# Sample keys loaded by pairs of sequences in 1 KB pieces, scored in one run, with early loads tied to the gate

## The chip, the cores and the metric

The kernel runs on one core of a Trainium2 chip. The core has a matmul engine (TensorE, PE in the profile, with its weight loads listed apart as PEld), a vector engine (VectorE, DVE), an engine for activations and copies (ScalarE, ACT), a general engine (GpSimd, POOL) and an engine that here only issues DMAs (SyncE, SP). Each engine runs its own instructions strictly in order and waits on semaphores for the others. DMAs are issued from the queues of SP (the weights) and of POOL (nearly all the rest) and share 16 DMA engines. The metric is the device time of one execution in microseconds.

## The reference

One inference step of a decoder layer for a prompt (1 sequence of 256 tokens) and a sample group (8 sequences of 4 tokens), with model width 2048, all in float32. The parts, in order: a projection to the inputs of two branches, a Mamba-2 (SSD) branch and a gated linear attention (GLA) branch, sigmoid gates that merge the two, cross-attention into 256 memory tokens, and a causal ConvFFN of width 5632. The change concerns the cross-attention of the sample group and what is loaded for it during the gate. That part of the reference is

```python
def _cross_attend(hn, mem_k, mem_v, w_cq, w_co):
    q = (hn @ w_cq).reshape(Bsz, L, CROSS_HEADS, CROSS_HEAD_DIM)
    s = jnp.einsum('blhd,bmhd->bhlm', q, mem_k) * (CROSS_HEAD_DIM ** -0.5)
    pr = jax.nn.softmax(s, axis=-1)
    o = jnp.einsum('bhlm,bmhd->blhd', pr, mem_v)
    return o.reshape(Bsz, L, D_MODEL) @ w_co
```

There are 4 heads of width 512. The prompt's memory keys and values are computed in the same step; those of the eight sample sequences are inputs (`cache_mem_k`, `cache_mem_v`, each 8 x 256 x 4 x 512), 4 MB of keys and 4 MB of values per head.

## The kernel before, in words

**Layout.** Activations lie with channels on the 128 partitions and the 288 tokens (256 of the prompt, then 32 of the sample group) along the free axis. Every large product is done in three passes: the weights and the activations are split into a rounded high part and a remainder, and high x high, high x low and low x high are summed. ScalarE writes the high part of a weight tile (`whi`, line 107), VectorE the remainder (`wlo`, line 109); both come in rings of five tiles. Raw weights (`raw`) come from SP's queue in 512 KB tiles, in a ring of three. One such tile of a projection of 256 columns serves 24 matmuls of 288 columns.

**Stages.** Memory keys and values of the prompt; input projection with the SSD and GLA scans woven in; output projections of the branches into `mb`; the gate stage (`gate_b`, which merges the branches, two channel tiles for each projection); the mix projection (`w_mix_out`), which adds the residual and writes `h_d`; the cross-attention; the output projection `w_co`; the ConvFFN.

**Order.** A planner puts the instructions of each engine in an order of its own, by a simulated time; within that, the code hands it the work woven together: `weave(main, bg, n_main, n_bg)` advances the background generator in proportion to the main one. In the cross-attention the main generator of head `hd` is the query projection of head `hd + 1` (16 steps of 12 matmuls), for the last head the first twelve steps of `w_co` (144 matmuls); the background generator is `attend(hd)`, with 20 steps. The DMAs that POOL issues for the attention are kept in program order.

**Loads of the attention.** `mem_load` takes a tile of 128 x 1024 floats from a ring of ten (`k4`, 40 KB a partition in all). A tile of sample keys holds one sequence: four DMAs of 128 KB put the four quarters of the head's 512 channels on four groups of 32 partitions, 128 channels (512 bytes) to a piece. A key tile is then turned by blocks of 32 x 32 on VectorE (`turn_keys`, two instructions of 512 columns), so that a partition holds a channel. Prompt keys (`kp`) and prompt values (`vp`) have tiles of their own; values of sequences 4 to 7 (`vc`) take tiles of the ring, those of sequences 0 to 3 (`vq`) a large buffer shared with other stages. Keys of head 0 are asked for in the gate stage, one sequence for every two gate tiles, `kp`, `vp` and `vq` in the mix stage. Nothing there but the ring ties a load to a time.

**Scores of the sample group.** A query tile of the projection is 128 channels x 32 rows. `diag` copies it into the block-diagonal tile `xqm` (one block of 32 columns per sequence, zero outside the sequence's own four). For each sequence and each of the four channel quarters a matmul with 32 stationary columns adds 256 scores; four sequences lie side by side on TensorE's columns. This is done in two halves: sequences 0 to 3, after which the values of 4 to 7 are loaded into their tiles, and sequences 4 to 7, after which keys 0 to 4 of the next head are. Key 5 follows the split of the prompt values, keys 6 and 7, `kp`, `vp` and `vq` follow the value products (line 1505).

The functions that the change touches are below.

Of the kernel before, what the change touches and what calls it, by code (L numbers as in the profile page):

```python
# [8 lines left out]
F32 = mybir.dt.float32  # L9
# [7 lines left out]
P = 128  # L17
# [25 lines left out]
def hybrid_step(ctx: ExitStack, tc: tile.TileContext, I: dict, O: list):  # L43
# [1218 lines left out]
    def mem_load(hd, kind, b=0):  # L1262

        t = pk.tile([P, 1024], F32, tag="k4", bufs=10, name={"k": "kc", "kp": "kp", "vp": "vp", "v": "vc"}[kind])
        if kind in ("k", "kp"):
            src = I["cache_mem_k"][b, :, hd, :] if kind == "k" else o_pmk[0, :, hd, :]
            for i in range(4):
                tc.keep_in_program_order(G.dma_start(
                    out=t[32 * i:32 * i + 32].rearrange("p (t x) -> p t x", x=P),
                    in_=src[:, i * P:(i + 1) * P].rearrange("(t m) x -> m t x", m=32)))  # L1270
        else:
            src = I["cache_mem_v"][b, :, hd, :] if kind == "v" else o_pmv[0, :, hd, :]
            tc.keep_in_program_order(G.dma_start(out=t.rearrange("p (m d) -> p m d", m=2),
                                                 in_=src.rearrange("(m p) d -> p m d", p=P)))
        ktiles[hd, kind, b] = t

    turned = set()

    def turn_keys(hd, kind, b=0):

        if (hd, kind, b) not in turned:
            turned.add((hd, kind, b))
            t = ktiles[hd, kind, b]
            for c in range(2):
                V.transpose(t[:, 512 * c:512 * c + 512], t[:, 512 * c:512 * c + 512])
# [17 lines left out]
    def gate_b(t, a):  # L1303
# [5 lines left out]
        if t % 2:  # L1309
            mem_load(0, "k", t // 2)  # L1310
# [35 lines left out]
    for j2 in range(KT // 2):  # L1346
# [6 lines left out]
        if j2 < 2:  # L1353
            mem_load(0, ("kp", "vp")[j2])
        elif j2 < 6:
            vq_load(0, j2 - 2)
# [17 lines left out]
    xqm = [px.tile([P, 4, NB, NS], F32, name=f"xqm{i}") for i in range(2)]  # L1374
# [16 lines left out]
    def q_proj(hd):  # L1391
# [5 lines left out]
        def evac(j):  # L1397
            if j % 2 == 0:
                qp.append((q2("qh"), q2("ql")))
            qs = px.tile([P, T], F32, tag="qs", bufs=1, name="qs")  # L1400
            V.tensor_tensor(qs, accs[j][:, 0:T], rc[0], ALU.mult)
            split(qp[j // 2][0][:, j % 2, :], qp[j // 2][1][:, j % 2, :], qs[:, 0:SEQ])
            diag(xqm[hd % 2][:, j], qs[:, SEQ:T])
# [20 lines left out]
    def keys(t):  # L1424
        return t.rearrange("p (t j m) -> p j t m", t=8, j=4)

    def attend(hd):

        xq = xqm[hd % 2]
        more = hd < 3  # L1430
        ssc = la_tile()

        def scores(q):
            for d in range(4):
                for j in (3, 2, 1, 0):
                    b = 4 * q + j
                    MM(ssc[NS * j:NS * j + NS, 0:256], xq[:, d, b, :], keys(ktiles[hd, "k", b])[:, d], start=(q == 0 and d == 0),
                       stop=(q == 1 and d == 3))

        for b in (4, 5):  # L1440
            turn_keys(hd, "k", b)
            yield
        scores(0)
        for b in range(4, NB):
            mem_load(hd, "v", b)
        yield
        for b in (6, 7):
            turn_keys(hd, "k", b)
            yield
        turn_keys(hd, "kp")  # L1450
        kh, kl = r4("kTh"), r4("kTl")
        kv = keys(ktiles[hd, "kp", 0])
# [25 lines left out]
        vp = ktiles[hd, "vp", 0].rearrange("p (m d) -> p m d", m=2)  # L1478
        vh, vl = v2("vph"), v2("vpl")
        split(vh, vl, vp)  # L1480
        if more:
            mem_load(hd + 1, "k", 5)
# [26 lines left out]
        if more:  # L1509
            for b in (6, 7):  # L1510
                mem_load(hd + 1, "k", b)
# [283 lines left out]
```

## Time and profile before

| | us |
|---|---|
| median of three runs | 2558.97 (2555.58 to 2562.18) |
| the profiled execution | 2558.26 |
| its span, first to last instruction | 2556.5 |
| TensorE busy | 2514.2 |
| VectorE busy | 1749.1 |
| ScalarE busy | 1332.6 |
| POOL busy | 459.4 |
| last GLA output projection and start of the gate | about 1195 to 1240 |
| gate, mix | up to about 1425 |
| cross-attention, first query matmul to last fold | 1424.8 to 1631.3 |

The profile is of one execution. Its views are a page, groups of instructions by line, waits, the DMA queues (q0 is POOL's, q1 SP's: packets, MB, share of the 16 engines), instructions in order of time, and busy time by stretches. In a row of the order of time stand the start and the length in us, the engine, the line, the operation, the tile written and the tiles read, the count, and in brackets the idle time before it with what ended it. In a row of groups stand count, busy us, mean ns, and idle time before. Matmuls overlap, so a length of 0.29 us does not mean that a matmul costs as much.

### The profile page before, as it was taken

How to read it: one execution, taken by the hardware profiler on the slowest of the kernel's cores; microseconds unless marked ns; L12 is line 12 of the kernel's file. 1: busy time of each engine (PE TensorE's matmuls, PEld its weight loads, DVE VectorE, ACT ScalarE, POOL GpSimd, SP SyncE). 2: the span in 40 equal slices, each digit the busy share in tenths (PEclk: the TensorE clock that was granted, in tenths of full speed). 3: DMA queues.
4: the chain of work that ended last, by engine and by line, in shares of the span. 5: the costliest groups of instructions: out<-in, count | busy, mean ns of one | idle time of the engine just before them, and what ended most of it. 6: DMA issues, size and time to landing. Idle time of an engine off the chain costs nothing.

```text
span 2556.5 us, 50096 instructions
## 1 busy us (share of the span) xinstructions
PE 2514.2 (98%) x18678; PEld 2412.1 (94%) x18678; DVE 1749.1 (68%) x3712; ACT 1332.6 (52%) x2680; POOL 459.4 (18%) x849
## 2 busy tenths in 40 slices
PE   9999999999999999999999999899999999999998
PEld 8889999989999999998999988799999999999998
DVE  6656777787767666765765567567777677675765
ACT  7656547645364555544454543356545455454545
POOL 3002234241200000012101155412010101020010
PEclk9999999999999999999999999999999999999999
DMA  8776587776868585778757699655555555555553
GB/s 265 218 223 200 170 243 212 226 209 191 233 195 286 175 255 165 245 235 245 213 180 250 199 288 284 216 170 173 167 173 168 173 167 174 168 170 171 169 172 128
DMA packets 435812, 521.93 MB, mean 204 GB/s; under 512 B 28860, under 2 KB 375836, under 8 KB 435504
## 3 DMA queue, kind: packets, MB, share of 16 engines
q1 hardware_dynamic: 399536, 422.34, 54.6%
q0 software_dynamic: 36000, 96.38, 12.8%
q8 instruction: 146, 2.39, 0.4%
q14 instruction: 98, 0.80, 0.1%
q10 hardware_dynamic: 32, 0.01, 0.0%
HBM read 473.13 MB, written 45.48 MB: 203 GB/s over the span
## 4 chain that ended last, share of the span: by engine, by line
PE 92%; DMA 4%; DVE 1%; POOL 1%; ACT 1%; issue 0%; SPq 0%; DVEq 0%; ACTq 0%; POOLq 0%
PE acc L152 25%; PE acc L151 25%; PE acc L155 25%; PE acc L319 2%; PE acc L320 2%; PE acc L323 2%; DMA raw<-in_w_in_dram 1%; PE acc L1417 1%; PE acc L1418 1%; PE acc L1419 1%; DMA kc<-in_cache_mem_k_dram 1%; PE mm L1151 1%; PE la L1142 1%; DMA raw<-in_w_cq_dram 1%; DMA raw<-in_w_gla_out_dram 1%; PE mm L1115 1%
## 5 line engine op out<-in xcount | busy, mean ns | idle before, releaser
L109 DVE TENSOR_TENSOR wlo<-raw,whi 128x512 fp32r<-128x512 f32 x1464 | 994.8, 687 | 656.0 <-ACT whi L107 645.4
L107 ACT CAST whi<-raw 128x512 fp32r<-128x512 f32 x1464 | 894.0, 618 | 1048.3 <-PE acc L152 741.2
L151 PE MATMUL acc<-xn,whi 128*128 128x288 f32 (+1 forms) x1936 | 550.3, 299 | 1.1 <-ACT whi L107 1.1
L152 PE MATMUL acc<-xn,whi 128*128 128x288 f32 (+1 forms) x1936 | 541.8, 295 | 0.0
L155 PE MATMUL acc<-xn,wlo 128*128 128x288 f32 (+1 forms) x1936 | 414.2, 295 | 0.0
L152 PE MATMUL acc<-hf,whi 128*128 128x288 f32 x1408 | 393.2, 295 | 0.0
L151 PE MATMUL acc<-hf,whi 128*128 128x288 f32 x1408 | 389.0, 292 | 0.0
L151 PEld LDWEIGHTS acc<-xn,whi 128*128 128x128 f32 (+1 forms) x1936 | 364.1, 188 | 11.7 <-issue 8.3
L152 PEld LDWEIGHTS acc<-xn,whi 128*128 128x128 f32 (+1 forms) x1936 | 364.4, 188 | 6.8 <-issue 4.8
L155 PEld LDWEIGHTS acc<-xn,wlo 128*128 128x128 f32 (+1 forms) x1936 | 310.3, 188 | 1.8 <-issue 1.1
L155 PE MATMUL acc<-hf,wlo 128*128 128x288 f32 x1408 | 294.5, 290 | 0.0
L152 PEld LDWEIGHTS acc<-hf,whi 128*128 128x128 f32 x1408 | 264.5, 188 | 0.1
L151 PEld LDWEIGHTS acc<-hf,whi 128*128 128x128 f32 x1408 | 264.0, 188 | 0.1
L155 PEld LDWEIGHTS acc<-hf,wlo 128*128 128x128 f32 x1408 | 226.2, 188 | 0.0
L152 PE MATMUL acc<-pr,whi 128*128 128x288 f32 x704 | 196.6, 295 | 0.0
L151 PE MATMUL acc<-pr,whi 128*128 128x288 f32 x704 | 195.0, 293 | 0.0
L1619 POOL COPY fsp<-fst 128x16 f32<-128x16 f32 x88 | 36.5, 416 | 650.4 <-DVE av L1631 426.8
L151 PE MATMUL acc<-un,whi 128*128 128x288 f32 x512 | 146.1, 301 | 7.2 <-DVE mb L959 5.7
L155 PE MATMUL acc<-pr,wlo 128*128 128x288 f32 x704 | 147.4, 290 | 0.0
L152 PE MATMUL acc<-un,whi 128*128 128x288 f32 x512 | 143.0, 295 | 0.0
L152 PEld LDWEIGHTS acc<-pr,whi 128*128 128x128 f32 x704 | 132.3, 188 | 0.0
L151 PEld LDWEIGHTS acc<-pr,whi 128*128 128x128 f32 x704 | 132.0, 188 | 0.0
(504 smaller groups left out, 4369.5 us busy)
## 6 DMA issues: line engine op xcount, KB each, us to landing
raw<-in_w_in_dram SPq DMA_DIRECT2D x240, 512.0 KB
raw<-in_w_up_dram SPq DMA_DIRECT2D x176, 512.0 KB
raw<-in_w_down_dram SPq DMA_DIRECT2D x88, 512.0 KB
raw<-in_w_cv_dram SPq DMA_DIRECT2D x32, 512.0 KB
raw<-in_w_ssd_out_dram SPq DMA_DIRECT2D x32, 512.0 KB
sin<-in_state_gla_dram POOLq DMA_DIRECT2D x32, 512.0 KB, 6.0
out_dram<-sin SPq DMA_DIRECT2D x32, 512.0 KB
raw<-in_w_gla_out_dram SPq DMA_DIRECT2D x32, 512.0 KB
```

The costliest lines, as they stand in the source:

```text
L107: S.copy(view(hi), raw)
L109: V.tensor_tensor(view(lo), raw, view(hi), ALU.subtract)
L151: MM(a, hi[:, k, cs], xh, start=(k0 + s0 + k == 0), stop=False)
L152: MM(a, hi[:, k, cs], xl, start=False, stop=False)
L155: MM(a, lo[:, k, cs], xh, start=False, stop=(k0 + s0 + k == nk - 1))
L319: MM(accs[m], mn_hi[:, kk, ms_], hi[:, 0, :], start=(kk == 0), stop=False)
L320: MM(accs[m], mn_lo[:, kk, ms_], hi[:, 0, :], start=False, stop=False)
L323: MM(accs[m], mn_hi[:, kk, ms_], lo[:, 0, :], start=False, stop=(kk == KT - 1))
L1115: MM(a, kt[:, i, k * P:(k + 1) * P], vt[i], start=True, stop=True)
L1142: MM(osa[NS * j:NS * j + NS, :], qdm[:, k, b, :], sins[b][:, k, :], start=False, stop=(q == 1 and k == 0))
L1151: MM(a, kb[:, k * P:(k + 1) * P], vst, start=True, stop=True)
L1619: G.tensor_copy(sp[:, :, 0:2], st.rearrange("p (b k) -> p b k", k=2))
```

## The change

- **Ring.** Ten tiles of 1024 columns become five of 2048 (`k8`). A key tile holds a pair of sequences, the prompt keys and prompt values of a head share one tile (`kvp`), and two sequences' values share one.
- **Pieces.** A key tile is filled by four DMAs of 256 KB: two sequences by two channel halves, each on 32 partitions, 256 channels (1 KB) to a piece. A partition group thus belongs to one sequence and one half of the channels. The turn is the same, in instructions of 1024 columns.
- **Scores.** A matmul covers a pair of sequences and 64 channels, eight steps for the 512 channels, four pairs side by side. All pairs are done in one run, and after it the values of sequences 4 to 7 and the first two key pairs of the next head are asked for. The third pair follows the split of the prompt values, the fourth and the prompt's rows follow the value products. The last two key pairs are turned at the start of the head that uses them, the first two in the head before.
- **Queries.** The layout needs query channels on other partitions than the projection leaves them. `evac` writes the 32 sample columns of each query tile to `qsm`; `spread` multiplies them by two 0/1 tiles `perm` (two products per head) and two copies put the result into `xqm`. The copies by `diag` go.
- **Early loads.** The four key pairs of head 0 are asked for after gate tiles 3, 7, 11 and 15, and before each a one-column copy on POOL from that gate tile into the key tile makes the load wait for it. Prompt rows and `vq` are asked for in the mix stage, as before, `vq` one step earlier.
- **Steps.** `attend` has 18 steps in head 0 and 22 in the others.

```diff
+    def ring(name):
+        return pk.tile([P, 2048], F32, tag="k8", bufs=5, name=name)
+    def key_load(hd, c, after=None):
+        t = ktiles[hd, "k", c] = ring("kc")
+        if after is not None:
+            G.tensor_copy(t[:, 0:1], after)
+        for s_ in range(2):
+            for dh in range(2):
+                r = 64 * s_ + 32 * dh
+                tc.keep_in_program_order(G.dma_start(
+                    out=t[r:r + 32].rearrange("p (t x) -> p t x", x=256),
+                    in_=I["cache_mem_k"][2 * c + s_, :, hd, 256 * dh:256 * dh + 256].rearrange("(t m) x -> m t x", m=32)))
+    def rows_load(hd):
+        t = ktiles[hd, "p"] = ring("kvp")
...
+    def turn32(t, c):
+        V.transpose(t[:, 1024 * c:1024 * c + 1024], t[:, 1024 * c:1024 * c + 1024])
...
-        if t % 2:
-            mem_load(0, "k", t // 2)
+        if t % 4 == 3:
+            key_load(0, t // 4, th[:, 0:1])
...
-            V.tensor_tensor(qs, accs[j][:, 0:T], rc[0], ALU.mult)
-            split(qp[j // 2][0][:, j % 2, :], qp[j // 2][1][:, j % 2, :], qs[:, 0:SEQ])
-            diag(xqm[hd % 2][:, j], qs[:, SEQ:T])
+            V.tensor_tensor(qsm[:, j], accs[j][:, SEQ:T], rc[0][:, SEQ:T], ALU.mult)
+            V.tensor_tensor(qs, accs[j][:, 0:SEQ], rc[0][:, 0:SEQ], ALU.mult)
+            split(qp[j // 2][0][:, j % 2, :], qp[j // 2][1][:, j % 2, :], qs)
...
+    def spread(xq):
+        a = mm_tile()
+        for jh in range(2):
+            MM(a[:, jh * P:(jh + 1) * P], perm[jh].rearrange("p s d x -> p (s d x)"), qsm.rearrange("p j t -> p (j t)"),
+               start=True, stop=True)
+        for s_ in range(2):
+            rows = slice(64 * s_, 64 * s_ + 64)
+            f, g = xq[rows].rearrange("p j c t -> p (j c t)"), a[rows, 0:256]
...
     def attend(hd):
+        spread(xq)
+        yield
+        if hd:
+            for c in (2, 3):
+                for h_ in range(2):
+                    turn32(ktiles[hd, "k", c], h_)
+                    yield
         ssc = la_tile()
...
-        scores(0)
-        for b in range(4, NB):
-            mem_load(hd, "v", b)
...
-        scores(1)
-        if more:
-            for b in range(5):
-                mem_load(hd + 1, "k", b)
+        for j in range(8):
+            for c in (3, 2, 1, 0):
+                kt = ktiles[hd, "k", c].rearrange("p (t j m) -> p j t m", t=8, j=8)
+                MM(ssc[NS * c:NS * c + NS, 0:256], xq[:, j, c, :], kt[:, j], start=(j == 0), stop=(j == 7))
+        for c in (2, 3):
+            val_load(hd, c)
+        if more:
+            for c in (0, 1):
+                key_load(hd + 1, c)
...
-        weave(main, attend(hd), 16 if hd < 3 else 12, 20)
+        weave(main, attend(hd), 16 if hd < 3 else 12, 22 if hd else 18)
```

More of the change, by code (lines that the diff above doesn't have):

```diff
@@ L1430, in attend @@
         more = hd < 3
-        ssc = la_tile()
[L1433 to L1442, printed above, removed]
-        scores(0)
-        for b in range(4, NB):
-            mem_load(hd, "v", b)
+        spread(xq)
[5 more added lines that the diff above has]
+                    yield
+        ssc = la_tile()
+        for j in range(8):
[7 more added lines that the diff above has]
+                key_load(hd + 1, c)
         yield
[L1447 to L1450, printed above, removed]
+        yield
+        kp = ktiles[hd, "p"]
+        turn32(kp, 0)
         kh, kl = r4("kTh"), r4("kTl")
-        kv = keys(ktiles[hd, "kp", 0])
+        kv = kp[:, 0:1024].rearrange("p (t j m) -> p j t m", t=8, j=4)
         for d2 in range(2):
```

73 lines of the change are left out of this document (35 added, 38 removed).

## The prediction

> **What bounds the kernel now.** I read the page first, then the busy time by stretches, then the waits, the DMA queues and the order of time inside the two stretches that the change touches.
>
> ```profile
> span 2556.5 us, 50096 instructions
> PE 2514.2 (98%) x18678; PEld 2412.1 (94%) x18678; DVE 1749.1 (68%) x3712; ACT 1332.6 (52%) x2680; POOL 459.4 (18%) x849
> PE 92%; DMA 4%; DVE 1%; POOL 1%; ACT 1%; issue 0%; SPq 0%; DVEq 0%; ACTq 0%; POOLq 0%
> ```
>
> TensorE is the bound: 98% busy, 92% of the chain that ended last. A change that leaves its arithmetic alone can only win back time in which TensorE stands still or runs at a lower clock, so the question is where it does so. By stretches (length, then busy us and instruction count of PE, PEld, DVE, ACT, POOL; the granted clock; the DMA share; GB/s):
>
> ```profile
> 1195.00:1200.00 5.00, 5.00 (x40) 5.00 (x40) 2.62 (x6) 1.13 (x2) 2.36 (x4) 1.00 1.01 372
> 1200.00:1205.00 5.00, 4.60 (x35) 4.36 (x34) 0.00 (x0) 0.00 (x0) 1.75 (x3) 1.00 1.06 270
> 1205.00:1210.00 5.00, 2.01 (x15) 2.04 (x16) 2.03 (x4) 1.14 (x2) 3.64 (x7) 1.00 1.08 260
> 1200.00:1220.00 20.00, 14.31 (x104) 13.69 (x104) 7.25 (x14) 4.56 (x8) 11.52 (x20) 1.00 1.07 268
> 1220.00:1240.00 20.00, 18.86 (x134) 17.58 (x133) 10.73 (x22) 7.94 (x16) 4.81 (x9) 1.00 0.94 238
> 1240.00:1260.00 20.00, 20.00 (x154) 20.00 (x154) 18.08 (x33) 10.21 (x19) 0.57 (x1) 1.00 0.74 215
> 1424.80:1631.30 206.50, 191.43 (x1549) 166.25 (x1547) 128.98 (x276) 82.61 (x164) 89.33 (x146) 0.98 0.85 249
> 1520.00:1540.00 20.00, 18.05 (x144) 15.03 (x143) 15.39 (x39) 10.01 (x22) 12.12 (x21) 1.00 1.02 260
> 1600.00:1620.00 20.00, 11.83 (x112) 9.46 (x110) 13.11 (x30) 5.27 (x12) 5.18 (x8) 0.91 0.81 298
> 1605.00:1631.30 26.30, 17.18 (x126) 12.38 (x126) 13.25 (x31) 6.69 (x16) 3.01 (x6) 0.87 0.45 175
> ```
>
> A stretch with nothing in the way holds 154 matmuls in 20 us, 0.130 us each (1240 to 1260). The two rows ahead of it, where the last GLA output projection goes over into the gate stage, hold 104 and 134: 70 short, 70 x 0.130 = 9.1 us lost. The cross-attention (1424.8 to 1631.3) loses 206.5 - 191.4 = 15.1 us idle, and a mean clock of 0.98 is another 4 us: about 19 us. Of that the end of the last head (last row) has 9.1 us idle and 26.3 x 0.13 = 3.4 us by the clock, 12.5 together; 1600 to 1620, with 11.8 us busy of 20, is the worst of it. So 28 us at most are to be had.
>
> What ends the wait at the gate: ScalarE, which splits the weights, waits for raw weight tiles (us in total, times, longest), while the queue of POOL moves 32 key tiles:
>
> ```profile
> ACT whi L107 <- DMA raw<-in_w_in_dram: 12.3, 4, 4.2
> ACT whi L107 <- DMA raw<-in_w_gla_out_dram: 12.1, 2, 8.4
> q0 software_dynamic: 1854, 5.59, 60.8%
> q1 hardware_dynamic: 3677, 3.65, 44.6%
> kc<-in_cache_mem_k_dram POOLq DMA_DIRECT2D x32, 128.0 KB, 7.1
> ...
> mar<-mg_d POOLq DMA_DIRECT2D x1, 576.0 KB, 8.6
> ```
>
> The middle three rows are the DMA view of 1195 to 1228, the last is that of 1192 to 1200: POOL's queue (q0) takes 60.8% of the engines, the weights (q1) get 3.65 MB in 33 us, 111 GB/s. TensorE eats one 512 KB tile in 24 matmuls, 24 x 0.130 = 3.1 us, 168 GB/s. That is the loss.
>
> In the cross-attention the key loads again hold the queue. DMA view of 1474 to 1502 (all 4.2 MB of one head's keys), then of 1502 to 1521 (prompt rows and values, 2 KB pieces), then the value issues of the first head (KB, us to landing):
>
> ```profile
> q0 software_dynamic: 1527, 4.20, 60.6%
> q1 hardware_dynamic: 1366, 2.63, 36.1%
> ...
> q0 software_dynamic: 1472, 5.15, 75.0%
> q1 hardware_dynamic: 936, 1.82, 27.5%
> ...
> vc<-in_cache_mem_v_dram POOLq DMA_DIRECT2D x3, 512.0 KB, 9.5
> ```
>
> Keys in 512-byte pieces: 4.20 MB / 28 us = 150 GB/s at a 0.606 share, 247 GB/s if they had all engines. Pieces of 2 KB: 5.15 / 19 = 271 GB/s at 0.75, 361 GB/s. So the piece length has a price of its own. In the last head this arrives too late:
>
> ```profile
> 1460.76 1.43 POOL L1273 DMA_DIRECT2D vc<-in_cache_mem_v_dram  x2 [29.14 <-PE la L1437]
> 1493.03 1.16 POOL L1268 DMA_DIRECT2D kc<-in_cache_mem_k_dram  x2 [0.45 <-DMA kc<-in_cache_mem_k_dram]
> 1601.48 1.93 PE L1437 MATMUL la<-kc,xqm 128*32 128x256 f32 x32
> 1609.72 3.37 PE L1437 MATMUL la<-kc,xqm 128*32 128x256 f32 x32 [4.80 <-DVE kc L1285]
> 1620.12 0.72 PE L1494 MATMUL mm<-ident,prp 128*128 128x128 f32 x4 [2.61 <-DVE prp L1386]
> 1624.17 0.41 PE L1522 MATMUL mm<-pTh,vph 128*128 128x256 f32 x1
> ```
>
> At 1609.7 TensorE waits 4.8 us for the last keys; by then the output projection that was to run beside the head has been used up, so softmax, transposes and values follow one another bare, and the matmuls go at the lower clock (0.41 us where L1522 has 0.28 elsewhere).
>
> **The change, part by part.** *Gate.* The 32 key DMAs of head 0 become 16 of 256 KB, and each group of four waits behind a one-column POOL copy of a gate tile (t = 3, 7, 11, 15). In the order of instructions of the changed kernel the copies stand on POOL between the loads of the staged merge tiles, and the first h_d store comes after all of them. Gate tiles are two projections apart, 16 x 12 matmuls x 0.130 = 25 us, so 1 MB comes every 25 us instead of 4 MB at once. What stays at the old place are the staged loads mar and hx, 2 x 576 and 3 x 288 KB, 2.0 MB. Bounds of the gain: 9.1 us if they cause none of the loss, 0 if they cause all. TensorE was full up to 1200 (40 matmuls in 5 us), with these loads under way since 1192, and short from 1205, when only keys were left (15); I take 8, near the upper end. Four bursts of 1 MB beside 168 GB/s of weights: at a 0.6 share each starves the weights by some 60 GB/s for 5.5 us, 2 us of weights, which the ring of three tiles (9.4 us) covers; without that cover it is at most 4 x 2 us. VectorE's turns of those keys stand seven weight splits behind the gate tile, about 11 us; copy, issue and landing take some 9 (four issues of 0.58 and the 7.1 above). Nothing, but close.
>
> *Pieces of 1 KB.* Between 247 (512 B) and 361 GB/s (2 KB) at full share. If a piece costs a fixed part and a part by length, the two ends (16 engines: 33.2 and 90.8 ns a piece) give 52 ns for 1 KB, 313 GB/s. Its share I put between the two measured and nearer the larger, 0.71, because a DMA carries twice the bytes of before: 222 GB/s, 4.2 MB in 19 us instead of 28. Bounds 17 and 28.
>
> *One run of scores.* The matmuls are as many as before (32 of 32 columns per head, two passes each, 1.93 us for 32). Before, half the scores of a head freed the tiles for the values and the other half those for the next keys. Now all five tiles of the ring come free late, and the chain of loads between two heads is serial: end of the scores, values of two pairs, four key pairs, prompt keys, turn, scores. By rows: values, issue to last landing 12.7 (three issues of 0.71 and the 9.5 and more above), keys 19, prompt keys (0.5 MB, still 512-byte pieces) 2 at nearly the whole share (3.5 at 150 GB/s). Then VectorE:
>
> ```profile
> L1285 DVE STREAM_TRANSPOSE kc<-kc 128x512 f32<-128x512 f32 x48 | 30.9, 686 | 6.1 <-DMA kc<-in_cache_mem_k_dram 6.1
> L1285 DVE STREAM_TRANSPOSE kp<-kp 128x512 f32<-128x512 f32 x6 | 3.9, 682 | 0.0
> L1401 DVE TENSOR_TENSOR qs<-acc,rstd 128x288 f32<-128x288 f32 x16 | 7.2, 447 | 1.1 <-PE acc L1419 0.8
> L198 DVE COPY xqm<-qs 128x32 f32<-128x32 f32 x16 | 2.8, 175 | 0.2
> L1417 PE MATMUL acc<-hn,whi 128*128 128x288 f32 x256 | 76.5, 301 | 0.0
> L1534 PE MATMUL mm<-fold,os 128*128 128x32 f32 x32 | 4.0, 268 | 0.0
> ```
>
> *The spread queries.* Per head two more products, four passes of 128 columns; the eight fold passes (L1534) end 1.08 us after they start, so about 0.5 us. On VectorE four small products and two copies replace four diagonal copies, each near the 0.175 us of L198: 0.4 us more, beside other work. But the order of instructions has a new dependence at each head's start: TensorE runs 14 matmuls of the next projection, then the spread, one more, then 19 scores, and VectorE has the last key pair's turn *ahead of* two of the small products, and the prompt keys' turn (2 x 0.68 = 1.4 us) *ahead of* the copies that fill xqm and of three of the four evacuations. Behind that turn, which waits for a DMA, stand TensorE's score run, three accumulator banks and all later weight splits. Before, scores were late without holding the projection up; now it stops. From the last landing to the scores: 1.4, and some 1.6 for small operations, 3 us.
>
> *Sum of the cross-attention.* TensorE's need: the projection is 192 matmuls (three lines of 256 for four heads), 25 us; 187.5 us of work (206.5 - 19) less 4 x 25 and 144 early output matmuls (19 us) leaves 17 per head: 42 us a head, 43 with the spread and its switches. The loop of loads: 45 matmuls between the pieces of the score run and the run itself (5.9 + 3.9, with switches 10.4), 12.7, 19, 2 (in the stall the weights stop and q0 nears the whole share), 3: 47 us. So each of three head starts stalls about 4 us: 12, with 2 more in the tail for softmax, and 2 for the clock after stalls: 16. In the tail the new order keeps 117 of the 144 output matmuls for after the spread of the last head, so softmax and value loads have cover: the 12.5 us go, apart from those 2. 19 us lost become 16: -3, bounds -12 (below) and +21 (rival 2).
>
> All in all -8 - 3 = -11 on the profiled run: its span 2556.5, with some 1.8 us around it, 2558.3; its median stands 0.7 higher, at 2559.0. That gives 2548.
>
> Of the pieces, the Trainium skill ("DMA: Bandwidth & Descriptors", Specifications) says that 512 bytes suffice for line rate, so that 1 KB would gain nothing; by it the keys keep their 28 us and the time is that of rival 2. The trace disagrees as far as it goes, 247 against 361 GB/s at full share for 512 B and 2 KB; 1 KB on POOL's queue it does not show.
>
> **The rivals.** *1. The keys gain more than half the way* (chance 0.17): they take 17 us or less, the loop is 45 or less, the stalls 0 to 2 each and too short for the clock, 7 lost in all with the tail: the cross-attention saves 12, with the gate 20: 2539. For it: fewer, larger DMAs (16 issues of 0.58 us instead of 32) keep twice the bytes in flight. Against: the share in the value stretch was won from the weights, and behind it, from 1520 to 1540, TensorE held 144 matmuls in 20 us.
>
> *2. The load chain holds TensorE at every head's start* (0.20), the one that ends on the other side: keys keep 28 us, the loop is 57; by the time TensorE has run out (43 us) 1.2 MB of keys and the prompt keys are missing, at 235 GB/s 7.4 us, and 3 for VectorE: 10.4 a head, 31, 3 for the tail, and after each stall some 2 us by the clock as in 1605 to 1631: 40 instead of 19, +21, less 8: +13, 2572. For it: VectorE's order as above, and that before the loads were already the slower chain (scores of the last head 4.8 us late). It decides from keys of some 20 us on, where the cross-attention breaks even; from about 23 the gate's 8 are eaten too.
>
> *3. The gate's loss stays* (0.15): mar and hx, not the keys, let the weights fall behind, or the bursts fall on the ring as hard. Then the cross-attention's -3 alone is left: 2556. Against: the keys hold 60.8% for another 25 us after those loads.
>
> **How the numbers follow.** The forecast's case has 0.48, its own range 2541 to 2556 (gate -6 to -9, cross -9 to +6). A measurement of this kernel tells about 0.3%, 7.7 us: faster is below 2551.3, slower above 2566.7. Faster: 0.38 of the 0.48 and all of rival 1, 0.55. Slower: 0.17 of rival 2. Same: the rest, 0.28. The range, 2534 to 2569, leaves out the faster part of rival 1 and the worse half of rival 2.
>
> **What would show it.** Right: TensorE holds about 154 matmuls per 20 us from 1200 to 1240, and no wait of ScalarE for w_in or w_gla_out above 2 us there; key DMAs of 256 KB, 4.2 MB of them in 18 to 20 us; TensorE idle 3 to 6 us in one piece at three head starts, ended by VectorE's turn of the prompt keys or the copy into xqm; little idle in the last 26 us. Wrong: a key stretch still 28 us long, or stalls of 10 us (rival 2); no stall at the head starts (rival 1); the gate short again (rival 3); weights that starve beside the larger pieces, seen as ScalarE waiting for w_cq in the middle of a head.

## The result: slower by 0.4%

The changed kernel takes 2567.9 us (median; 2566.5 to 2570.2). Beside it the kernel before takes 2559.1, and the ratio is 1.0037 (95% interval 1.0024 to 1.0050). The prediction was 2548 with a range of 2534 to 2569: the time lies just inside the range, on the other side of the kernel before than forecast. The profiled execution has a span of 2565.1 us against 2556.5, 8.6 longer. The head of its page, with the chain that ended last:

```profile
span 2565.1 us, 49979 instructions
...
PE 2523.2 (98%) x18694; PEld 2422.4 (94%) x18694; DVE 1750.1 (68%) x3686; ACT 1331.1 (52%) x2680; POOL 424.1 (17%) x789
...
PE 90%; DMA 6%; DVE 3%; issue 1%; POOL 0%; ACT 0%; SPq 0%; DVEq 0%; ACTq 0%
```

DMA and VectorE rose from 4% and 1% of that chain to 6% and 3%. By stretches (columns as in the prediction's rows; the fourth is the whole cross-attention, from the first matmul of the first query projection to the end of the last fold):

```profile
1200.00:1220.00 20.00, 19.39 (x148) 19.18 (x147) 13.59 (x25) 8.51 (x14) 0.00 (x0) 1.00 0.64 189
1220.00:1240.00 20.00, 20.00 (x155) 20.00 (x154) 13.04 (x25) 11.27 (x21) 0.99 (x3) 1.00 0.54 159
1340.00:1360.00 20.00, 18.57 (x139) 18.14 (x138) 11.72 (x22) 8.30 (x18) 1.83 (x3) 1.00 0.77 242
1415.23:1639.81 224.58, 200.76 (x1564) 176.59 (x1562) 130.79 (x259) 81.50 (x164) 66.74 (x108) 0.93 0.82 235
1480.00:1500.00 20.00, 13.74 (x91) 12.60 (x93) 15.93 (x29) 4.78 (x13) 5.91 (x9) 0.72 1.04 299
1501.00:1511.00 10.00, 10.00 (x84) 7.67 (x78) 3.63 (x8) 3.21 (x6) 0.17 (x1) 0.93 0.11 34
1540.00:1560.00 20.00, 11.96 (x80) 10.29 (x80) 17.30 (x32) 3.81 (x9) 6.49 (x10) 0.75 1.00 275
1557.00:1567.00 10.00, 10.00 (x90) 8.60 (x85) 4.54 (x10) 3.73 (x7) 0.00 (x0) 0.83 0.34 112
1613.00:1639.80 26.80, 26.80 (x250) 22.15 (x248) 14.39 (x34) 11.28 (x24) 9.37 (x17) 1.00 0.76 253
```

The gate is healed: 148 and 155 matmuls where 104 and 134 stood. The cross-attention begins at 1415.2 instead of 1425.0, 9.7 us earlier, and takes 224.6 us instead of 206.4, 18.2 longer; 18.2 - 9.7 = 8.5, the whole difference of the spans. In it TensorE is idle for 23.8 us (224.58 - 200.76) against 15.1, and its mean clock is 0.93 against 0.98: 200.8 x 0.07 = 14 us against 4. The loss stands at the head starts: 1480 to 1500 and 1540 to 1560 have 13.7 and 12.0 us busy at a clock of 0.72 and 0.75. Right behind them (1501 to 1511, 1557 to 1567) the DMA engines are little used, at a share of 0.11 and 0.34. The tail (last row) is full at full clock.

The DMA view of the key loads, of 1465 to 1485, then of 1524 to 1544:

```profile
q0 software_dynamic: 1006, 3.29, 67.8%
q1 hardware_dynamic: 885, 1.71, 36.0%
```
```profile
q0 software_dynamic: 1080, 3.54, 79.5%
q1 hardware_dynamic: 557, 1.07, 24.1%
```

3.29 MB in 20 us are 165 GB/s, at a share of 0.678: 243 GB/s at full share. The second row gives 177 at 0.795, 223. Pieces of 1 KB cost the engines as much per byte as pieces of 512 B did.

Waits in the cross-attention (1425 to 1645), in total, times, longest; first of the changed kernel, then the wait for weights of the kernel before in the same stretch:

```profile
DVE kc L1296 <- DMA kc<-in_cache_mem_k_dram: 26.3, 9, 7.3
ACT whi L107 <- DMA raw<-in_w_cq_dram: 23.1, 7, 5.0
```
```profile
ACT whi L107 <- DMA raw<-in_w_cq_dram: 21.0, 11, 6.6
```

The weights are late about as much as before. VectorE waits 26.3 us for keys, where the kernel before has 6.1. What stands behind such a wait shows in order of time, at the start of the second head (VectorE; TensorE; the loads of the values of the four heads on POOL; and 1490 to 1500 by stretches):

```profile
1485.59 2.37 DVE L1296 STREAM_TRANSPOSE kc<-kc 128x1024 f32<-128x1024 f32 x2 [2.07 <-DMA kc<-in_cache_mem_k_dram]
...
1489.81 0.42 DVE L1418 TENSOR_TENSOR qs<-acc,rstd 128x256 f32<-128x256 f32 x1
...
1491.99 2.37 DVE L1296 STREAM_TRANSPOSE kc<-kc 128x1024 f32<-128x1024 f32 x2 [1.67 <-DMA kc<-in_cache_mem_k_dram]
...
1494.29 0.25 DVE L1417 TENSOR_TENSOR qsm<-acc,rstd 128x32 f32<-128x32 f32 x2
...
1495.58 1.24 DVE L1296 STREAM_TRANSPOSE kvp<-kvp 128x1024 f32<-128x1024 f32 x1
1496.74 0.55 DVE L1449 COPY xqm<-mm 64x128 f32<-64x128 f32 x2
```
```profile
1490.38 0.58 PE L1433 MATMUL acc<-hn,whi 128*128 128x288 f32 x1 [4.36 <-DVE qs L1418]
...
1494.59 1.22 PE L1444 MATMUL mm<-qsm,perm 128*128 128x128 f32 x4 [0.52 <-DVE qsm L1417]
...
1497.35 4.69 PE L1467 MATMUL la<-kc,xqm 128*32 128x256 f32 x38 [1.30 <-DVE xqm L1449]
...
1509.48 1.07 PE L1467 MATMUL la<-kc,xqm 128*32 128x256 f32 x16
```
```profile
1453.69 2.85 POOL L1291 DMA_DIRECT2D vc<-in_cache_mem_v_dram  x4 [34.64 <-PE la L1467]
...
1510.83 2.83 POOL L1291 DMA_DIRECT2D vc<-in_cache_mem_v_dram  x4 [17.26 <-PE la L1467]
...
1568.09 2.83 POOL L1291 DMA_DIRECT2D vc<-in_cache_mem_v_dram  x4 [16.43 <-PE la L1467]
...
1617.09 2.83 POOL L1291 DMA_DIRECT2D vc<-in_cache_mem_v_dram  x4 [11.02 <-PE la L1467]
```
```profile
1490.00:1495.00 5.00, 4.11 (x16) 3.79 (x17) 3.33 (x7) 1.09 (x3) 2.13 (x3) 0.50 1.03 281
1495.00:1500.00 5.00, 3.70 (x30) 3.23 (x33) 4.67 (x11) 1.67 (x4) 0.00 (x0) 0.50 1.03 414
```

The first evacuation of the queries (qs, 1489.81) stands behind a pair's turn, the next ones and the spread products behind the next pair's turn, the copies into xqm behind the prompt keys' turn. TensorE stops three times in 12 us, runs at half clock until 1500, and ends the score run at 1510.5, 16 us after the last pair was turned (1494.4). Only then do ring tiles come free, and the loads of the values start at 1510.8. In the whole cross-attention (1425 to 1645) TensorE waits 11.3 us for what VectorE writes from the queries (`qs`, `qsm`, `xqm`); the longest of these waits:

```profile
PE acc L1433 <- DVE qs L1418: 4.4, 1, 4.4
PE mm L1444 <- DVE qsm L1417: 3.1, 2, 2.6
PE la L1467 <- DVE xqm L1449: 3.1, 2, 1.8
```

### The profile page after: what moved, and what is told of

It is laid out like the page before. It is cut to its first block, busy times and chain, and to the rows that moved or that the text cites. A ratio compares the mean times of both kernels' runs of the same rounds, so it can differ in the third digit from the quotient of the medians.

```text
span 2565.1 us, 49979 instructions
## 1 busy us (share of the span) xinstructions
PE 2523.2 (98%) x18694; PEld 2422.4 (94%) x18694; DVE 1750.1 (68%) x3686; ACT 1331.1 (52%) x2680; POOL 424.1 (17%) x789
## 4 chain that ended last, share of the span: by engine, by line
PE 90%; DMA 6%; DVE 3%; issue 1%; POOL 0%; ACT 0%; SPq 0%; DVEq 0%; ACTq 0%
PE acc L152 25%; PE acc L151 25%; PE acc L155 24%; DMA kc<-in_cache_mem_k_dram 2%; PE acc L319 2%; PE acc L320 2%; PE acc L323 2%; DMA raw<-in_w_mix_out_dram 1%; DMA vc<-in_cache_mem_v_dram 1%; PE la L1467 1%; DVE wlo L109 1%; PE acc L1433 1%; PE acc L1435 1%; PE acc L1434 1%; PE mm L1151 1%
```

## Experiments

Ratios are against the kernel before, run beside each kernel on the same chip; the changed kernel's is 1.0037.

**What the price of a key load depends on** (e1 to e4). e1 keeps pieces of 1 KB and DMAs of 256 KB and lets each DMA write all 128 partitions:

```
             for dh in range(2):
-                r = 64 * s_ + 32 * dh
+                o = 512 * (2 * s_ + dh)
...
-                    out=t[r:r + 32].rearrange("p (t x) -> p t x", x=256),
-                    in_=I["cache_mem_k"][2 * c + s_, :, hd, 256 * dh:256 * dh + 256].rearrange("(t m) x -> m t x", m=32)))
+                    out=t[:, o:o + 512].rearrange("p (t x) -> p t x", x=256),
+                    in_=I["cache_mem_k"][2 * c + s_, :, hd, 256 * dh:256 * dh + 256].rearrange("(t m) x -> m t x", m=P)))
```

> Each key DMA still carries 256 KB in 1 KB pieces, but to all 128 partitions (2 pieces a partition) instead of 32 (8 pieces a partition). The keys then lie in another order in the tile, so the decode scores are those of a shuffled key matrix; every instruction and every byte stays. Theory P (partitions: the key loads are slow because a DMA writes only 32 partitions, whatever the piece length): key DMAs reach 340 to 360 GB/s at full share as the value loads do, 4.2 MB of keys take about 15 us instead of about 24, each of three head starts comes 8 us earlier, time 2543 to 2550. Theory L (length: 1 KB pieces cost what 512-byte pieces cost, only 2 KB pieces are cheap): keys stay at about 243 GB/s at full share, time 2563 to 2573.

e2 keeps the 32 partitions and lengthens the pieces to 2 KB, e3 shortens them to 512 B, each in the same few lines (x=512 with whole rows; a loop over two blocks of 128 columns):

> Each key DMA still carries 256 KB to 32 partitions, but as four whole rows of 2 KB a partition instead of eight pieces of 1 KB. The keys lie in another order in the tile, so the decode scores are those of a shuffled key matrix; every instruction and every byte stays. Theory L (length): 360 GB/s at full share, time 2543 to 2550. Theory P (partitions): 240 to 250 GB/s at full share as with 512 B and 1 KB, time 2563 to 2573.

> The changed kernel with its key pairs loaded in eight DMAs of 128 KB in 512-byte pieces, as the kernel before cut them, into the same layout; all else stays. My prediction's price (247 GB/s at full share for 512 B, 313 for 1 KB) would make this about 5 us a head slower than the changed kernel, 2580 to 2585. Theories P and L, as the trace of the changed kernel has it (243 GB/s for 1 KB): the pieces make no difference, 2564 to 2574, the twelve extra issues of 0.58 us a head lying behind full DMA engines.

e4 swaps the two loops, so that neighbouring DMAs write different halves of the partitions:

```
-        for s_ in range(2):
-            for dh in range(2):
+        for dh in range(2):
+            for s_ in range(2):
```

> The changed kernel with one thing changed: the four DMAs of a key pair go to partitions 0, 64, 32, 96 in turn instead of 0, 32, 64, 96. The instructions of all engines stay. Theory P with neighbouring DMAs overlapping: two DMAs in flight now write different halves of the partitions, keys at 280 GB/s or more at full share, time 2550 to 2560. Theory P with DMAs served one after the other, and theory L: no difference, 2565 to 2571. The Trainium skill ("SBUF — State Buffer", Door 1) has partitions 0 to 63 share one half of the ports and 64 to 127 the other; no run so far shows it.

Measured (in e1 and e2 the keys lie in another order in the tile, so their scores are not the reference's): e1 2536.4 us, ratio 0.9912 (0.9897 to 0.9927); e2 2568.0, 1.0037 (1.0023 to 1.0052); e3 2568.3, 1.0033 (1.0021 to 1.0046); e4 2563.7, 1.0020 (1.0011 to 1.0029). The DMA views of the key stretch of the second head, e1 (1515 to 1527), e2 (1525 to 1543), e3 (1527 to 1547):

```profile
q0 software_dynamic: 1118, 3.64, 78.0%
q1 hardware_dynamic: 563, 1.09, 24.3%
```
```profile
q0 software_dynamic: 967, 3.17, 78.5%
```
```profile
q0 software_dynamic: 1005, 2.73, 60.9%
q1 hardware_dynamic: 848, 1.63, 33.0%
```

At full share that is 389 GB/s for e1 (3.64 MB / 12 us / 0.780), 224 for e2 and 224 for e3, beside 223 of the changed kernel in the same head. To 32 partitions, pieces of 512 B, 1 KB and 2 KB cost nearly the same; to 128 partitions, 1 KB costs 0.58 of that. Between these four runs the price goes by the partitions that a DMA writes, not by its pieces. This is what the Trainium skill ("SBUF — State Buffer", Door 1) has: a range of 32 partitions reaches half of the 16 ports; the runs agree, 224 against 389 GB/s, though the rate is 0.58 and not a half. Whether the twice larger DMAs win share is not settled: e3's 0.609 takes in a stretch at its end in which the engines were not full (from 1541 on), and over equal stretches the changed kernel has 0.668 against 0.572 in the first head (1468 to 1482) and 0.695 against 0.691 in the second (1527 to 1541). The time is the same. e4 lies 4 us under the changed kernel, between the two forecasts, with 255 GB/s at full share (3.62 MB in 18 us at 0.790), as if neighbours overlapped a little; the overlap itself was not looked at.

**The gate** (e5, e6, e11). e5 is the kernel before with the tie alone; e6 the changed kernel without it; e11 is e5 with the prompt keys' turn kept behind what is written ahead of it.

In e5 (`mem_load` makes the copy that the changed kernel's `key_load` makes), in e6, and in e11, where v is the turn:

```
-            mem_load(0, "k", t // 2)
+            mem_load(0, "k", t // 2, th[:, 0:1])
```
```
-            key_load(0, t // 4, th[:, 0:1])
+            key_load(0, t // 4)
```
```
+                if kind == "kp":
+                    tc.keep_in_program_order(v)
```

> The kernel before with one part of the change alone: each of the eight key loads of head 0 waits behind a one-column copy of its gate tile; pieces, ring, scores and queries stay as before. Theory G (the keys of head 0 starve the weights at the gate, and the tie ends that at no cost): TensorE holds about 152 matmuls or more in each 20 us from 1200 to 1240 and the time is 2549 to 2553, 6 to 10 us under before. Rival (the loss moves to where the keys then land, or their turns hold VectorE): 2555 to 2560.

> The changed kernel without the tie: the four key pairs of head 0 are loaded as soon as their ring buffers stand free. Theory G: the gate's loss comes back, 8 to 10 us, less some 2 us that the changed kernel loses at 1340 to 1360: 2574 to 2578. Rival (the larger pieces, not the tie, relieved the gate): 2565 to 2571.

> The kernel before with the tied key loads, as in the run of the gate alone, and its prompt keys' turn pinned on VectorE behind what is written ahead of it. In the run of the gate alone VectorE waited 7.6 us for the prompt keys at 1341 to 1349 and the 8 us won at the gate were lost there. Theory G2 (that turn alone took the gain back): 2549 to 2553. Rival (the cross-attention is bound by its loads, which end when they end, so that an earlier start of the stage is spent waiting): 2555 to 2559.

Measured: e5 2557.3, ratio 0.9995 (0.9983 to 1.0007); e6 2580.3, 1.0082 (1.0059 to 1.0105); e11 2557.4, 1.0006 (0.9994 to 1.0018). e6 first, then e5, by stretches, and VectorE in e5 in order of time:

```profile
1200.00:1220.00 20.00, 10.07 (x49) 9.69 (x50) 6.06 (x12) 3.04 (x6) 5.84 (x10) 0.81 1.06 236
1220.00:1240.00 20.00, 19.64 (x126) 19.33 (x127) 10.23 (x20) 8.49 (x15) 0.00 (x0) 0.85 0.70 187
```
```profile
1200.00:1220.00 20.00, 18.96 (x142) 18.75 (x141) 13.53 (x25) 8.90 (x16) 0.00 (x0) 1.00 0.64 173
1345.00:1350.00 5.00, 1.88 (x15) 1.64 (x13) 1.24 (x3) 0.41 (x1) 0.00 (x0) 1.00 0.35 76
```
```profile
1348.76 1.30 DVE L1287 STREAM_TRANSPOSE kp<-kp 128x512 f32<-128x512 f32 x2 [7.58 <-DMA kp<-out_dram]
```

In the changed kernel the tie is worth some 12 us (2580.3 against 2567.9): without it only 49 matmuls are left in the first 20 us. In the kernel before it heals the gate too, and wins nothing. Part of the gain goes at once: the prompt keys' turn now stands early in VectorE's order and waits 7.6 us, with the weight splits behind it. e11 takes that wait away and the time stays. But there VectorE waits 20.5 us (1195 to 1425) for the tied keys themselves, where the kernel before has no such wait, and TensorE is idle for 3.3 us from 1300 to 1340:

```profile
DVE kc L1287 <- DMA kc<-in_cache_mem_k_dram: 20.5, 6, 5.7
```

So its cross-attention starts only 3.9 us earlier than that of the kernel before (1421.1), and it ends at 1632.1, 0.8 later. I read this as a stage that waits for its loads and gives an earlier start back; which of its waits does so was not tried. It is no rule: the stage of the changed kernel starts 12.0 us earlier than that of e6 (1427.2) and is only 1.7 us longer (224.6 against 222.9), so there the gain is kept.

**Why the cross-attention is 18 us longer.** The price of the keys is the same in both kernels, so it can't be that alone. e7 cuts the score run in two; e12 makes one run of the two in the kernel before; e8 and e13 change VectorE's and TensorE's order at the head starts; e14 does both.

In turn e7, e12, e8 and e13 (mm is a score matmul; `scores(cs)` runs the eight steps for the pairs named; `keep_in_program_order` ties an instruction to the one written just before it on its engine):

```
+        scores((1, 0))
+        for c in (2, 3):
+            val_load(hd, c)
...
+        scores((3, 2))
```
```
             for d in range(4):
-                for j in (3, 2, 1, 0):
-                    b = 4 * q + j
+                for b in (3, 2, 1, 0, 7, 6, 5, 4):
+                    j = b % 4
```
```
-                    turn32(ktiles[hd, "k", c], h_)
+                    tc.keep_in_program_order(turn32(ktiles[hd, "k", c], h_))
...
-        turn32(kp, 0)
+        tc.keep_in_program_order(turn32(kp, 0))
```
```
+                if hd and j == 0:
+                    tc.keep_in_program_order(mm)
```

> The changed kernel with its one score run cut in two: pairs 0 and 1 first, behind which the values are loaded, then pairs 2 and 3. Theory S (the serial loop: all ring buffers come free at the end of one score run, the DMA engines stand idle for about 10 us at each of three head starts, and with keys at 180 GB/s the loop is longer than TensorE's need): the value loads start about 10 us earlier in each head, the idle stretches of the DMA engines halve or better, and the time is 2540 to 2558; two strips of TensorE at once instead of four may give back up to 4 us a head. Theory V (VectorE's order at the head starts holds TensorE): no change, 2563 to 2573.

> The kernel before with one part of the change alone: the two half runs of scores become one, block by block over all eight sequences, so that all eight key tiles come free only at its end; pieces of 512 bytes, queries, ring of ten tiles and the early loads stay. Theory S (one run makes the loop of loads between two heads serial): the DMA engines stand idle for 8 to 12 us at each of three head starts, the starts of the score runs lie 55 to 60 us apart, the cross-attention takes 12 to 25 us longer and the time is 2571 to 2584. Rival (the loop is as long with half runs, because keys at 150 to 180 GB/s alone set it): 2555 to 2565.

> The changed kernel with VectorE's order at the head starts mended: the prompt keys' turn stands behind the copies that fill xqm and behind the evacuations of its head, and the turns of pairs 2 and 3 behind what is written ahead of them. Theory V: a wait for the prompt keys no longer stops the evacuations; 2556 to 2562. Theory S: the loop of loads is as long as before, the stall only moves, 2564 to 2571.

> The changed kernel with the score runs of heads 1 to 3 kept behind what is written ahead of them on TensorE: the 32 matmuls of a run stand in one piece behind 46 matmuls of the next projection in place of starting behind 13, and end where they ended. Theory O (TensorE's order: the changed kernel stops TensorE for keys that a better order would have covered with projection matmuls, and the projection then lies inside the score run, which ends late and leaves the DMA engines idle for 10 us): up to 6 us a head of the stop is covered, DMA idle per head falls from about 10 to about 5, time 2550 to 2560. Rival (the stop comes from VectorE and the weights, not from where the scores stand): 2563 to 2570.

> The changed kernel with both orders mended: VectorE's turns as in the run of the late turns, TensorE's score runs as in the run of the pinned scores. Theory O with V: the evacuations pass, 46 projection matmuls cover the last turns, and the cross-attention comes down to what the loads take, about 14 MB a head at 300 GB/s: 2545 to 2556. Rival: as the late turns alone, 2558 to 2564.

Measured: e7 2572.4, ratio 1.0054 (1.0038 to 1.0069); e12 2559.9, 1.0016 (1.0000 to 1.0032); e8 2561.5, 1.0014 (1.0003 to 1.0025); e13 2568.2, 1.0043 (1.0027 to 1.0060); e14 2562.4, 1.0009 (0.9993 to 1.0024). The theory that one score run makes the loop of loads serial is borne out on neither side. Cutting the run frees its first tiles 4 and 7 us earlier in the second and third head (value loads at 1506.6 and 1561.4) and wins no time; its second half ends later, at 1517.5 instead of 1510.5. One run alone leaves the stage of the kernel before as long as it was, 205.8 us (row below) against 206.4. That row is of the fastest of ten executions; by the interval one run can cost up to 8 us, not the 12 to 25 of the theory. TensorE's order alone does nothing. VectorE's order is worth some 6 us, although the pin was a weak one, and some turns still stood ahead of evacuations. How long VectorE waits for keys in all does not order the runs: 26.3 us in the changed kernel, 14.2 in e7, which is slower, 20.2 in e8 and 26.5 in e14, which are both faster. TensorE's wait for `qs`, `qsm` and `xqm` hardly moved in these two either (10.6 and 10.5 us instead of 11.3), so where their 6 us come from stays open. So two runs moved the turns behind all evacuations of the queries and the copies into xqm, with the score run in one piece as in e13: all turns of a head (e16), or those of pairs 2 and 3 and of the prompt keys (e17).

```profile
1423.18:1629.02 205.84, 190.51 (x1548) 167.86 (x1546) 129.38 (x276) 82.20 (x164) 88.84 (x146) 0.97 0.86 250
```

The lines of e17; e16 also takes the turns of pairs 0 and 1 out of the loop of the value products:

```
+    def turn_behind(t, c):
+        with tc.issue_after(last["qs"].ins), tc.issue_after(last["xqm"].ins):
+            turn32(t, c)
...
-                    turn32(ktiles[hd, "k", c], h_)
+                    turn_behind(ktiles[hd, "k", c], h_)
...
-        turn32(kp, 0)
+        turn_behind(kp, 0)
```

> The changed kernel with all eight half turns of a head's key pairs and the prompt keys' turn behind the evacuations of the queries and the copies into xqm on VectorE, and the score runs of heads 1 to 3 in one piece behind some 65 matmuls of the next projection on TensorE. Theory W (VectorE's waits for keys, 26 us in the cross-attention of the changed kernel against 6 in the kernel before, are the stop of TensorE): no wait for keys stands ahead of an evacuation, TensorE ends each projection and goes on with the next, the cross-attention comes near the 206 us of the kernel before, time 2548 to 2557. Rival D (the loop of loads alone: from the last landing to the end of the scores it is as long as before, 16 to 19 us, while the ring is full and the DMA engines idle): 2560 to 2570.

> As the run with all turns behind, but only the turns of pairs 2 and 3 and of the prompt keys are moved; those of pairs 0 and 1 stay between the value products of the head before, where VectorE waited up to 7 us for them. Theory W: between the changed kernel with late turns and the run with all turns behind, 2552 to 2561. Rival D: as that run or better, since four turns less stand between the last landing and the scores, 2556 to 2566.

Measured: e16 2559.4, ratio 0.9998 (0.9985 to 1.0011); e17 2553.4, 0.9976 (0.9961 to 0.9990). The cross-attention of e17, and its waits for keys:

```profile
1414.69:1623.88 209.19, 193.49 (x1564) 171.09 (x1562) 130.29 (x260) 80.59 (x164) 63.34 (x102) 0.96 0.85 249
```
```profile
DVE kc L1296 <- DMA kc<-in_cache_mem_k_dram: 10.8, 4, 4.4
```

209.2 us instead of 224.6: 15.4 of the 18.2 are back, with the same pieces and ring and all scores in one run, and the time falls under that of the kernel before. TensorE's wait for `qs`, `qsm` and `xqm` falls from 11.3 us to 1.7. e13 shows that the pinned scores alone are not it; the moved turns without the pin were not tried. The head starts of e17 (rows as for the changed kernel above), the longest wait that is left on TensorE there, then the longest of e16:

```profile
1480.00:1500.00 20.00, 13.99 (x89) 13.04 (x89) 11.25 (x27) 3.99 (x10) 5.89 (x9) 0.83 1.03 296
1540.00:1560.00 20.00, 20.00 (x180) 18.22 (x179) 16.23 (x30) 7.44 (x16) 9.17 (x14) 0.92 1.01 328
```
```profile
PE acc L1439 <- ACT whi L107: 5.3, 1, 5.3
```
```profile
PE mm L1498 <- ACT kTh L192: 14.7, 2, 8.0
```

In e17 the third head's start is full, 20.0 us busy where 12.0 were. The second is not: there TensorE waits 5.3 us for a weight split. In e16 TensorE waits only 1.5 us for `qs`, `qsm` and `xqm`, but all eight half turns, 9.1 us in a row from 1492.2 on, and the prompt keys' turn stand ahead of the scores, TensorE waits 14.7 us for the prompt keys, and the cross-attention takes 218.1 us again. So 15 of the 18 us go with the order of VectorE's turns, the scores being pinned. In the trace TensorE's waits for the query tiles fall by 9.6 us and its idle time in all by 8.1 (23.8 to 15.7), and the clock rises from 0.93 to 0.96, which is worth some 6 (14 against 193.5 x 0.04 = 8). What the other 3 us are was not tried.

**Fast keys with the scores of the reference, without and with the orders** (e9, e10, e15, e18). In e9 a tile holds 256 dimensions of four sequences; partition 32 b + m has rows 8 m to 8 m + 7 of sequence b, so that one stride in memory covers all 128 partitions. e10 adds the pinned turn of the prompt keys, e15 the pinned scores, e18 both orders of e17. Of e9's lines:

```
+        q, h = divmod(c, 2)
+        src = I["cache_mem_k"][4 * q:4 * q + 4, :, hd, 256 * h:256 * h + 256].rearrange("b (m t) x -> (b m) t x", t=8)
+        for i in range(4):
+            tc.keep_in_program_order(G.dma_start(
+                out=t.rearrange("p (t x) -> p t x", x=256)[:, 2 * i:2 * i + 2], in_=src[:, 2 * i:2 * i + 2]))
...
+                MM(a2[0:64, 0:256], halfsum.rearrange("p q t -> p (q t)"), sb, start=True, stop=True)
```

> The changed kernel with its keys cut so that every key DMA writes all 128 partitions and the scores are the reference's again: a tile holds 256 of the 512 dimensions of four sequences, partition 32 b + m has the rows 8 m to 8 m + 7 of sequence b, pieces stay 1 KB and DMAs 256 KB. The eight steps of a tile contract 32 dimensions each, the two halves of the dimensions are added by one more product, and the queries are spread by four products instead of two. Theory P with the loop of loads as the bound: keys at 370 to 400 GB/s at full share as in the run with shuffled keys, the starts of the score runs 41 to 49 us apart, and 1 to 3 us a head for the added products and copies at most, largely beside other work: 2534 to 2546. Rival (the added chain of copy, product and softmax behind the scores is on the path): 2546 to 2556.

> The kernel of the quads with the prompt keys' turn pinned on VectorE behind what is written ahead of it (the copies into xqm and the evacuations), in the first head and the later ones. Theory V beside P (an early turn that waits for a DMA stops VectorE, and with it the weight splits, also where the keys come fast): 2 to 6 us under the quads alone, of it 2 at the mix projection (1340 to 1360). Rival (with fast keys the prompt keys have landed by the time of the turn): within 2 us of the quads alone.

> The kernel of the quads with its score runs of heads 1 to 3 in one piece behind 46 projection matmuls. Theory O: the DMA engines, idle for 7 us a head there, idle less, 2528 to 2534. Rival (with keys at 370 GB/s the loads no longer set the length of a head): 2534 to 2540.

> The kernel of the quads with the orders of the run that won most: turns of the last two key tiles and of the prompt keys behind the evacuations and the copies into xqm, score runs in one piece. Theory W: nothing more is to be had here, since VectorE waits only 0.5 us for keys when they come at 370 GB/s; within 3 us of the quads with pinned scores, 2530 to 2536. Rival (the order costs whatever the price of the keys): 2522 to 2530.

Measured: e9 2536.7, ratio 0.9929 (0.9911 to 0.9947); e10 2536.6, 0.9929 (0.9912 to 0.9946); e15 2533.1, 0.9902 (0.9887 to 0.9917); e18 2531.1, 0.9894 (0.9876 to 0.9911). The DMA view of e9's keys (1508 to 1522) and its cross-attention:

```profile
q0 software_dynamic: 1239, 4.13, 74.7%
```
```profile
1415.99:1612.93 196.94, 192.81 (x1588) 168.52 (x1586) 132.07 (x270) 83.85 (x168) 71.80 (x107) 0.99 0.78 267
```

295 GB/s, 395 at full share, and a stage of 196.9 us at a clock of 0.99: the kernel is some 18 us under the kernel before (0.0071 of 2559) and, by the ratios, some 28 under the changed one (1.0037 - 0.9929), with three more products a head. VectorE waits 0.5 us for keys. Its order is now worth little: the late turn nothing (e10), the pinned scores perhaps 3 us (e15, 0.9902 against 0.9929, intervals overlapping), the whole set of orders wins 2 us on the pinned scores (e18 against e15, intervals overlapping), where at slow keys e17 against e13 is 0.9976 against 1.0043.

## Why the prediction was wrong, step by step

- **Gate: right.** Predicted -8, with 154 matmuls in each 20 us; measured 148 and 155, and a stage that starts 9.7 us earlier. "Nothing, but close" held for VectorE's turns of these keys: VectorE waited 7.1 us for them in four pieces, and TensorE stayed full (20.00 of 20 us in each stretch from 1220 to 1340). What I had not priced is the prompt keys' turn behind them, which waits 5.8 us for its DMA: 2 us lost at 1340 to 1360 (139 of 154).
- **Pieces of 1 KB: the first step that failed.** I took 313 GB/s at full share from a line through 512 B and 2 KB, and so 19 us for a head's keys. It is 223 to 243, and 4.2 MB take 23 to 25 us (165 and 177 GB/s). The two ends differed in two things, length and partitions, and I gave all of it to the length; e1 to e3 show that it belongs to the partitions (224 GB/s at each length, 389 to all 128). The rule of the Trainium skill that I set against it ("DMA: Bandwidth & Descriptors", Specifications: 512 B suffice) was right that 1 KB wins nothing, and my reason for doubting it, 247 against 361, was the partitions. The share was about right: 0.71 forecast, 0.68 to 0.80 measured.
- **One run of scores: right place, wrong size, and half of its reason wrong.** The new dependence that I described, turns ahead of the evacuations and of the xqm copies, is most of the loss (e17). But I priced the loop as 47 us with stalls of 4. From one head's value loads to the next are 57, 57 and 49 us (1453.7, 1510.8, 1568.1, 1617.1). In the first of these loops the loads hold most of the excess: 38.3 us from the issue of the values to the end of the last wait for keys (1453.69 to 1491.99), where the sum had 12.7 + 19 = 31.7. Then come 5.4 from that turn's start to the first scores (1491.99 to 1497.35), where it had 2 for the prompt keys and 3, and 13.2 for the run instead of 10.4 (1497.3 to 1510.5), with TensorE at half clock up to 1500. The other half, that a ring which comes free at once makes the loads serial, the experiments do not bear out (e7, e12).
- **Clock: the second mis-sized term.** I gave 2 us for all heads. The two rows of 20 us at 0.72 and 0.75 alone cost 13.7 x 0.28 = 3.8 and 12.0 x 0.25 = 3.0, and the whole stage 10 us more than before.
- **Tail: right.** 26.8 of 26.8 us busy at full clock; the 12.5 us did go.
- **The sum.** Gate -9.7 and cross-attention +18.2 instead of -8 and -3. This is rival 2 (+21 - 8, 2572) nearly to the number, and with half of its mechanism: keys at the old price, and TensorE held at the head starts. But rival 2 had the length of the load chain hold it, and e17, with the same loads, gets most of the loss back by VectorE's order with the scores pinned. With VectorE's order left as it was, faster keys do it too (e9: 196.9 us). Rival 2 had 0.20. I had written its two conditions out of rows and then put the likeliest price of the keys just under the value from which it decides.

## What to carry to other kernels

Before a slow transfer is given longer pieces, two transfers that differ only in the pieces have to be compared; here the rate went by the number of partitions that a DMA writes, and a layout in which one stride covers 128 partitions won what longer pieces could not. A wait on an in-order engine costs what stands behind it: a turn that waits for a DMA belongs behind the evacuations that TensorE waits for, but no further back than that needs (in e16 TensorE then waited 14.7 us for the prompt keys), and where a planner makes the order, the order has to be read for such pairs. Time won ahead of a stage that waits for its loads may be lost again in it: the same tie was worth 12 us in the changed kernel and nothing in the kernel before.

## What the runs showed of the hardware that I had not expected

To 32 partitions, 512 B, 1 KB and 2 KB pieces all ran at 223 to 243 GB/s at full share in the stretches above, and the weights of the other queue slowed with them: at full share they ran at 222 and 238 GB/s beside the changed kernel's keys (1.07 MB in 20 us at 0.241, 1.71 MB in 20 us at 0.360), against 374 beside e1's (1.09 MB in 12 us at 0.243). Both queues together moved 251 and 231 GB/s in the changed kernel, against 396 while e1 loaded the same keys to 128 partitions.
